# S5 stage: input and scan-operator loads set ahead of output operators, both swaps of a pair ahead of its scans, loads lent the idle weight buffers

## The chip, the cores and the metric

One Trainium2 core runs the whole program. The metric is the device time of one launch in microseconds (us), as the median of repeated runs. TensorE multiplies matrices (PE; its weight loads are PEld), VectorE (DVE) and ScalarE (ACT) do elementwise work, GpSimd (POOL) does small fills and issues some DMAs, SyncE (SP) issues most DMAs. Each engine takes its own instructions in order.

## What is computed

A two-layer decoder trunk on x of 512 tokens by 1024 features, all in fp32. Layer 0 is FFN, Mamba-2 mixer, FFN; layer 1 is FFN, S5 mixer, FFN. The change is in the S5 mixer alone:

```
lam_bar = exp(lam * step);  b_bar = ((lam_bar - 1) / lam) * b
u = rmsnorm(x).reshape(L, 64 groups, 16)
h[t] = lam_bar * h[t-1] + b_bar @ u[t]          (64 complex states a group)
y[t] = real(c @ h[t]) + d * u[t];  g = gelu(y)
val, gate = split(g @ glu_w + glu_b);  x = x + val * sigmoid(gate)
```

## The kernel before

**Stages.** `f1_0, ssd, f2_0, f1_1, s5, f2_1` run one after the other. An fp32 product is taken as three matmuls of rounded halves (hi*hi, hi*lo, lo*hi; lines 235 to 237). In the FFNs the weight halves lie in the pools `whi` and `wlo`, three buffers each of 128 x 8 x 128 fp32; inside the S5 stage nothing needs them until the GLU weights 4 and up are split.

**S5 in tiles.** The 64 groups are cut into eight blocks i of eight groups, worked in pairs (0,1), (2,3), (4,5), (6,7). Time is cut into 64 steps of 8 tokens. For a block:

- `u_load(i)` fetches the block's input U (128 x 8 x 64) from a DRAM scratch `d_u`, in runs of 64 fp32; `scan_ops(i, n)` fetches the operator `opH` and, for n = 2, the table `tb`, into a ring of five buffers; `out_ops(i, h)` fetches the output operators `opP`, half h, into five buffers. All go through SP's queue.
- `states(i)`: DVE multiplies U by the norm's factor (line 1401), then 16 pairs of matmuls on PE give the step inputs in PSUM (line 1407).
- `scan(i)`: ACT copies the two halves of that PSUM tile crosswise into z2 (the *swap*, lines 1417 and 1418); DVE forms z1 and z2 with the table (1419, 1420), adds them (1421), runs the recurrence (1423), and after two more crosswise copies on ACT (1427, 1428) rotates the states back: v1 = z*tb, z2*tb, v1 - z2 (1429 to 1431). POOL fills rh and the first column of v1.
- `mix(i, h, w)` for a pair (i, i+1), half h: PE adds the direct part from U (w = 128) and the part from v1 (w = 0) (line 1440); ACT takes the gelu (1448).
- `channels(i)`: PE transposes the pair's gelu output (1460), ACT and DVE cut it into halves gh and gl (1464, 1465).
- `glu_k(i)`: twelve matmuls that add block i into four GLU outputs, whose weights are resident. GLU weights 4 and up (`glu_load`, POOL's queue) are split on ACT (226) and DVE (228).

**Order.** In this stage the order on PE, SP and POOL is the order of the code; on ACT and DVE a scheduler chooses it when the program is built. PE's order is states 0, 1; mix 0 (U); states 2; mix 0 (v); states 3; channels 0; then for the pairs from (4,5): states of the pair, mix of the pair before, two glu_k, channels. `ahead(i)` issues the loads: the four opP of pair (i, i+1), and behind them U, opH and tb of the next pair. An opP buffer comes free when the mix that read it is done. PSUM lends this stage four `aux` tiles.

Of the kernel before, what the change touches and what calls it, by code (L numbers as in the profile page):

```python
# [9 lines left out]
F32 = mybir.dt.float32  # L10
# [6 lines left out]
T = 512  # L17
D = 1024
KD = 8
# [11 lines left out]
def trunk_kernel(ctx, tc, x, ffn1_norm, ffn1_w_in, ffn1_w_out, mix_norm, ffn2_norm, ffn2_w_in, ffn2_w_out,  # L31
# [3 lines left out]
    nc = tc.nc  # L35
    V, S, G, PE = nc.vector, nc.scalar, nc.gpsimd, nc.tensor

    const = ctx.enter_context(tc.tile_pool(name="const", bufs=1))
    wpool = ctx.enter_context(tc.tile_pool(name="wpool", bufs=3))
# [8 lines left out]
    def aux_ps():  # L48
        return psum.tile([128, 512], F32, tag="aux", name="aux", bufs=4)
# [59 lines left out]
    def col(nm, j=0, n=1):  # L109
        i, r0 = C[nm]  # L110
        return cols[i][:, r0 + j:r0 + j + n]
# [864 lines left out]
    s5 = {}  # L976
# [347 lines left out]
    fl = lambda a: a.rearrange("p g k -> p (g k)")  # L1324
    gs8 = lambda i: slice(i * 8, i * 8 + 8)
    s5_in, s5_out = {}, {}
# [3 lines left out]
    def scan_ops(i, n):  # L1330

        w = s5_w.setdefault(i, [])
        while len(w) < n:
            if w:
                t_ = s5["ring"].tile([128, 2, 8, 64], F32, tag="ut", name="tb", bufs=5)
                nc.sync.dma_start(t_, s5["t"][i])
            else:
                t_ = s5["ring"].tile([128, 8, 128], F32, tag="ut", name="opH", bufs=5)
                nc.sync.dma_start(t_, s5["H"][:, gs8(i)])
            w.append(t_)  # L1340
        return w

    def u_load(i):

        if i not in s5_in:
            U = s5["op"].tile([128, 8, 64], F32, name="U", bufs=4)
            nc.sync.dma_start(U, s5["u"][i].rearrange("(g c) q k -> (c q) g k", c=16))
            s5_in[i] = U
        return s5_in[i]

    def out_ops(i, h):

        if (i, h) not in s5_out:
            P_ = s5["op"].tile([128, 4, 256], F32, name="opP", bufs=5)
            nc.sync.dma_start(P_, s5["P"][:, i * 8 + h * 4:i * 8 + h * 4 + 4])
            s5_out[i, h] = P_
        return s5_out[i, h]
# [32 lines left out]
    def s5_stage(pr, nxt):  # L1390
        with ExitStack() as es:
            sp = es.enter_context(tc.tile_pool(name="s5", bufs=2))
# [3 lines left out]
            pbs, ins, pys = {}, {}, {}  # L1396

            def states(i):

                U, W = u_load(i), scan_ops(i, 1)[0]  # L1400
                V.tensor_tensor(U, U, rL[:, None, :].to_broadcast([128, 8, 64]), op=OP.mult)
                pb = pbs[i] = aux_ps()
                for g in range(8):
                    s = slice(g * 64, g * 64 + 64)
                    for hf in range(2):
                        m = slice(hf * 64, hf * 64 + 64)
                        PE.matmul(pb[m, s], W[:, g, m], U[:, g], start=True, stop=True)

            def scan(i):

                pb, tb = pbs[i], scan_ops(i, 2)[1]
                rh = sp.tile([128, 8, 64], F32, name="rh", bufs=2)
                G.memset(rh[:, :, 0:1], 0.0)
                G.tensor_copy(rh[:, :, 1:], s5["rho"][:, gs8(i)][:, :, None].to_broadcast([128, 8, 63]))
                z1 = sp.tile([128, T], F32, name="z1", bufs=1)
                z2 = sp.tile([128, 8, 64], F32, name="z2")
                S.copy(fl(z2)[0:64], pb[64:128])
                S.copy(fl(z2)[64:128], pb[0:64])
                V.tensor_tensor(z1, pb, fl(tb[:, 0]), op=OP.mult)
                V.tensor_tensor(fl(z2), fl(z2), fl(tb[:, 1]), op=OP.mult)  # L1420
                V.tensor_tensor(z1, z1, fl(z2), op=OP.add)
                z = sp.tile([128, 8, 64], F32, name="z", bufs=1)
                V.tensor_tensor_scan(fl(z), fl(rh), z1, 0.0, op0=OP.mult, op1=OP.add)
                v1 = ins[i] = sp.tile([128, 8, 64], F32, name="v1", bufs=3)
                v2 = sp.tile([128, 8, 64], F32, name="z2")
                G.memset(v1[:, :, 0:1], 0.0)
                S.copy(v2[0:64, :, 1:64], z[64:128, :, 0:63])
                S.copy(v2[64:128, :, 1:64], z[0:64, :, 0:63])
                V.tensor_tensor(v1[:, :, 1:64], z[:, :, 0:63], tb[:, 0, :, 0:63], op=OP.mult)
                V.tensor_tensor(v2[:, :, 1:64], v2[:, :, 1:64], tb[:, 1, :, 0:63], op=OP.mult)  # L1430
                V.tensor_tensor(v1[:, :, 1:64], v1[:, :, 1:64], v2[:, :, 1:64], op=OP.subtract)

            def mix(i, h, w):

                if w:
                    pys[i, h] = aux_ps()
                py = pys[i, h]
                for g in range(4):
                    for e in range(2):
                        PE.matmul(py[e * 64:e * 64 + 64, g * 128:g * 128 + 128],  # L1440
                                  (u_load(i + e) if w else ins[i + e])[:, h * 4 + g],
                                  out_ops(i + e, h)[:, g, w:w + 128], start=bool(w) and g == 0,
                                  stop=not w and g == 3, skip_group_check=True)
                if w:
                    return
                if h == 0:
                    pys["gy"] = sp.tile([128, 8, 8, 16], F32, name="gy", bufs=1)
                S.activation(pys["gy"][:, :, h * 4:h * 4 + 4].rearrange("p q g c -> p g q c"),
                             py.rearrange("p (g q c) -> p g q c", g=4, q=8), AF.Gelu_apprx_tanh)
# [19 lines left out]
            def glu_k(i):  # L1469
                for j in range(2 * NR):  # L1470
                    hi, lo = res[j]
                    proj(rps[j], (hi[i // 4][:, i % 4:i % 4 + 1], lo[i // 4][:, i % 4:i % 4 + 1]), GH[i:i + 1],
                         GL[i:i + 1], first=i == 0, last=i == KD - 1)

            def glu_out(d, pv, pg):
                sg = sp.tile([128, T], F32, tag="z2", name="sg")
                S.activation(sg, pg, AF.Sigmoid, bias=col("gb", 8 + d))
                V.scalar_tensor_tensor(sg, pv, col("gb", d), sg, op0=OP.add, op1=OP.mult)
                new = s5.pop("spare")
                xv, sv = [a_.rearrange("p (q k) -> p k q", q=8) for a_ in (xT[d], sg)]  # L1480
                V.tensor_tensor(new.rearrange("p (k q) -> p k q", q=8), xv, sv, op=OP.add)
                s5["spare"], xT[d] = xT[d], new
                nxt.take(d)
                if d == KD - 1:
                    S.copy(s5["spare"], xT[1])
                    xT[1] = s5["spare"]

            def ahead(i):

                if i < KD:  # L1490
                    for h in range(2):
                        out_ops(i, h)
                        out_ops(i + 1, h)
                if i + 2 < KD:
                    for j in (i + 2, i + 3):
                        u_load(j)
                        scan_ops(j, 2)

            raw = {}

            def glu_load(*js):
                for j in js:
                    raw[j] = fetch_w(glu_cols(j), KD, eng=G)[0]
# [2 lines left out]
                states(i)  # L1506
            for h in range(2):
                mix(0, h, 128)
            scan_ops(2, 2)
            scan_ops(3, 1)  # L1510
            scan(0)
            scan(1)
            scan_ops(3, 2)
            states(2)
            for h in range(2):
                mix(0, h, 0)
            states(3)
            ahead(2)
            scan(2)
            channels(0)  # L1520
            scan(3)
            for i in range(4, KD + 2, 2):
                if i < KD:
                    states(i)
                    states(i + 1)
                for h in range(2):
                    mix(i - 2, h, 128)
                    mix(i - 2, h, 0)
                ahead(i)
                if i < KD:  # L1530
                    scan(i)
                    scan(i + 1)
                if i == KD - 2:
                    glu_load(4, 5)
                glu_k(i - 4)
                glu_k(i - 3)
                channels(i - 2)
# [7 lines left out]
            for d in range(NR):  # L1545
                glu_out(d, rps[2 * d], rps[2 * d + 1])
# [64 lines left out]
    with tc.manual_schedule(engines={mybir.EngineType.Activation, mybir.EngineType.DVE, mybir.EngineType.PE}):  # L1611
        xps, w = {}, {}
# [75 lines left out]
    for i, s in enumerate(stages[:-1]):  # L1688
# [5 lines left out]
        elif s == "s5":  # L1694
            with tc.manual_schedule(engines={mybir.EngineType.PE, mybir.EngineType.SP, mybir.EngineType.Pool}):
                s5_stage(pr, nxt)
# [75 lines left out]
```

## Time and profile before

| | |
|---|---|
| timed runs | 2053.25 us median of 3 (2051.19 to 2054.72) |
| the profiled execution | 2049.33 us, its span 2047.6 us, mean granted clock 0.989 |
| busy over the span | PE 1990.9 us, DVE 1494.4, ACT 943.5, POOL 223.3 |
| S5 stage | PE's first state matmul at 1537.09 us, its transposes of the last pair at 1611.45 us |

Times in the text are us from the start of the span. A row of the timeline reads: start, length, engine, line, operation, output <- input, shape, count, and in brackets the idle time before it with what ended it. A row of the chain of waits reads: start, length, what ran or what was waited for. A row of a table by windows gives busy time and count by engine (PE, PEld, DVE, ACT, POOL), the granted TensorE clock, the DMA share and the GB/s.

### The profile page before, as it was taken

How to read it: one execution, taken by the hardware profiler on the slowest of the kernel's cores; microseconds unless marked ns; L12 is line 12 of the kernel's file. 1: busy time of each engine (PE TensorE's matmuls, PEld its weight loads, DVE VectorE, ACT ScalarE, POOL GpSimd, SP SyncE). 2: the span in 40 equal slices, each digit the busy share in tenths (PEclk: the TensorE clock that was granted, in tenths of full speed). 3: DMA queues.
4: the chain of work that ended last, by engine and by line, in shares of the span. 5: the costliest groups of instructions: out<-in, count | busy, mean ns of one | idle time of the engine just before them, and what ended most of it. 6: DMA issues, size and time to landing. Idle time of an engine off the chain costs nothing. (4 is left out here: it accounts for less than half of the span.)

```text
span 2047.6 us, 32113 instructions
## 1 busy us (share of the span) xinstructions
PE 1990.9 (97%) x12477; PEld 1730.1 (84%) x12477; DVE 1494.4 (73%) x2677; ACT 943.5 (46%) x1613; POOL 223.3 (11%) x338
## 2 busy tenths in 40 slices
PE   8999999999999999999999999999985999999997
PEld 7887778888888887889999978999975888999996
DVE  6899986687875787776676667666767556866675
ACT  5324334465663565444444534444444433444453
POOL 1002322012111010000011000000101100100010
PEclk9999999999999999999999999999997999999999
DMA  7446675343334322355566327455766432654561
GB/s 188 121 122 166 166 192 129 96 118 121 111 101 121 103 84 68 106 148 122 120 149 153 93 85 171 118 120 128 189 197 218 132 103 72 166 138 112 131 141 67
DMA packets 410057, 265.47 MB, mean 130 GB/s; under 512 B 40008, under 2 KB 383088, under 8 KB 409904
## 3 DMA queue, kind: packets, MB, share of 16 engines
q1 hardware_dynamic: 383024, 202.60, 35.4%
q0 software_dynamic: 26560, 59.75, 14.0%
q8 instruction: 98, 1.61, 0.3%
q10 hardware_dynamic: 320, 1.06, 0.1%
q14 instruction: 55, 0.45, 0.1%
HBM read 215.06 MB, written 21.04 MB: 115 GB/s over the span
## 5 line engine op out<-in xcount | busy, mean ns | idle before, releaser
L226 ACT CAST whi<-wst 128x1024 fp32r<-128x1024 f32 (+3 forms) x354 | 315.5, 893 | 380.0 <-PE mm L236 291.2
L228 DVE TENSOR_TENSOR wlo<-wst,whi 128x1024 fp32r<-128x1024 f32 (+3 forms) x354 | 363.8, 1028 | 125.1 <-ACT whi L226 123.4
L235 PE MATMUL mm<-hH,whi 128*128 128x512 f32 x984 | 389.8, 396 | 0.0
L236 PE MATMUL mm<-hL,whi 128*128 128x512 f32 x984 | 384.6, 391 | 1.8 <-DVE hL L182 1.7
L237 PE MATMUL mm<-hH,wlo 128*128 128x512 f32 x984 | 383.9, 390 | 0.0
L237 PE MATMUL mm<-ah,wlo 128*128 128x512 f32 x704 | 274.8, 390 | 0.0
L235 PE MATMUL mm<-ah,whi 128*128 128x512 f32 x704 | 274.5, 391 | 0.0
L236 PE MATMUL mm<-al,whi 128*128 128x512 f32 x704 | 274.4, 390 | 0.0
L236 PEld LDWEIGHTS mm<-hL,whi 128*128 128x128 f32 x984 | 185.2, 188 | 41.1 <-DVE hL L182 3.0
L237 PEld LDWEIGHTS mm<-hH,wlo 128*128 128x128 f32 x984 | 184.9, 188 | 39.7 <-DVE wlo L228 0.4
L235 PEld LDWEIGHTS mm<-hH,whi 128*128 128x128 f32 x984 | 185.0, 188 | 39.4 <-issue 1.6
L384 PE MATMUL mm<-th,hH 128*128 128x256 f32 x612 | 173.5, 284 | 0.0
L386 PE MATMUL mm<-th,hL 128*128 128x256 f32 x612 | 173.2, 283 | 0.0
L385 PE MATMUL mm<-tl,hH 128*128 128x256 f32 x612 | 173.1, 283 | 0.0
L237 PEld LDWEIGHTS mm<-ah,wlo 128*128 128x128 f32 x704 | 132.2, 188 | 27.9 <-issue 0.6
L236 PEld LDWEIGHTS mm<-al,whi 128*128 128x128 f32 x704 | 132.3, 188 | 26.6 <-issue 0.2
L235 PEld LDWEIGHTS mm<-ah,whi 128*128 128x128 f32 x704 | 132.3, 188 | 26.0
L299 POOL DMA_DIRECT2D wu<-wst x51 | 43.2, 847 | 829.5 <-DMA wst<-in_ffn_w_in_dram 266.6
L384 PEld LDWEIGHTS mm<-th,hH 128*128 128x128 f32 x612 | 117.4, 192 | 2.4 <-ACT up L458 2.4
L385 PEld LDWEIGHTS mm<-tl,hH 128*128 128x128 f32 x612 | 117.4, 192 | 0.0
L386 PEld LDWEIGHTS mm<-th,hL 128*128 128x128 f32 x612 | 117.4, 192 | 0.0
L386 PE MATMUL mm<-th,wlo 128*128 128x256 f32 x408 | 115.5, 283 | 0.0
(393 smaller groups left out, 3918.9 us busy)
## 6 DMA issues: line engine op xcount, KB each, us to landing
wst<-in_ffn_w_in_dram SPq DMA_DIRECT2D x125, 512.0 KB, 4.5
wu<-in_ffn_w_in_dram SPq DMA_DIRECT2D x51, 512.0 KB, 5.9
wst<-in_ssd_in_proj_dram SPq DMA_DIRECT2D x48, 512.0 KB, 3.9
wst<-in_ffn_w_out_dram SPq DMA_DIRECT2D x72, 256.0 KB, 2.9
wst<-in_ffn_w_out_dram SPq DMA_DIRECT2D x48, 320.0 KB, 3.2
wu<-wst POOLq DMA_DIRECT2D x51, 256.0 KB, 4.5
ws<-wst POOLq DMA_DIRECT2D x51, 256.0 KB, 4.7
dec<-d_cs POOLq DMA_DIRECT2D x16, 512.0 KB, 4.5
```

The source lines that it names most:

```text
L226: S.copy(hi, st)
L228: V.tensor_tensor(lo, st, hi.bitcast(F32), op=OP.subtract)
L235: PE.matmul(ps, hi[:, k], H[k], start=first and k == 0, stop=False)
L236: PE.matmul(ps, hi[:, k], L[k], start=False, stop=False)
L237: PE.matmul(ps, lo[:, k], H[k], start=False, stop=last and k == n - 1)
L299: G.dma_start(dst, src, accum_op=OP.add)
L384: PE.matmul(ps[:, c0], hi[:, k], mh, start=first and k == 0, stop=False, skip_group_check=True)
L385: PE.matmul(ps[:, c0], hi[:, k], ml, start=False, stop=False, skip_group_check=True)
L386: PE.matmul(ps[:, c0], lo[:, k], mh, start=False, stop=k == 3, skip_group_check=True)
```

## The change

In SP's queue U and opH of blocks 4 and 5 are issued right behind the loads of blocks 2 and 3, ahead of opP for pair (2,3); the loads of 6 and 7 follow that opP, and `ahead` is left as `next_out`, which loads opP alone. opH of 4 and 5 and both U of 6 and 7 go into the three `whi` buffers, opH of 6 and both tables of 6 and 7 into the three `wlo` buffers. `swap(i)` is cut out of `scan(i)`, and both swaps of a pair are called ahead of its two scans; z2 gets three buffers instead of two. PE's order stays. Line numbers move: 1401 is 1407, 1407 is 1413, 1417 to 1431 are 1424 to 1445, 1440 is 1454, 1465 is 1479.

```diff
@@ -1331,19 +1331,25 @@
 
         w = s5_w.setdefault(i, [])
         while len(w) < n:
-            if w:
-                t_ = s5["ring"].tile([128, 2, 8, 64], F32, tag="ut", name="tb", bufs=5)
-                nc.sync.dma_start(t_, s5["t"][i])
+            nm, shape = ("tb", [128, 2, 8, 64]) if w else ("opH", [128, 8, 128])
+            tag = {(4, 0): "whi", (5, 0): "whi", (6, 0): "wlo", (6, 1): "wlo", (7, 1): "wlo"}.get((i, len(w)))
+            if tag:
+                t_ = wpool.tile(shape, F32, tag=tag, name=nm, bufs=3)
             else:
-                t_ = s5["ring"].tile([128, 8, 128], F32, tag="ut", name="opH", bufs=5)
-                nc.sync.dma_start(t_, s5["H"][:, gs8(i)])
+                t_ = s5["ring"].tile(shape, F32, tag="ut", name=nm, bufs=5)
+            nc.sync.dma_start(t_, s5["t"][i] if w else s5["H"][:, gs8(i)])
             w.append(t_)
         return w
 
     def u_load(i):
 
         if i not in s5_in:
-            U = s5["op"].tile([128, 8, 64], F32, name="U", bufs=4)
+            if i < 6:
+                U = s5["op"].tile([128, 8, 64], F32, name="U", bufs=4)
+            elif i == 6:
+                s5_in["last"] = wpool.tile([128, 2, 8, 64], F32, tag="whi", name="U", bufs=3)
+            if i >= 6:
+                U = s5_in["last"][:, i - 6]
             nc.sync.dma_start(U, s5["u"][i].rearrange("(g c) q k -> (c q) g k", c=16))
             s5_in[i] = U
         return s5_in[i]
@@ -1406,23 +1412,31 @@
                         m = slice(hf * 64, hf * 64 + 64)
                         PE.matmul(pb[m, s], W[:, g, m], U[:, g], start=True, stop=True)
 
-            def scan(i):
-
-                pb, tb = pbs[i], scan_ops(i, 2)[1]
+            swapped = {}
+
+            def swap(i):
+
+                pb = pbs[i]
                 rh = sp.tile([128, 8, 64], F32, name="rh", bufs=2)
                 G.memset(rh[:, :, 0:1], 0.0)
                 G.tensor_copy(rh[:, :, 1:], s5["rho"][:, gs8(i)][:, :, None].to_broadcast([128, 8, 63]))
-                z1 = sp.tile([128, T], F32, name="z1", bufs=1)
-                z2 = sp.tile([128, 8, 64], F32, name="z2")
+                z2 = sp.tile([128, 8, 64], F32, name="z2", bufs=3)
                 S.copy(fl(z2)[0:64], pb[64:128])
                 S.copy(fl(z2)[64:128], pb[0:64])
+                swapped[i] = rh, z2
+
+            def scan(i):
+
+                pb, tb = pbs[i], scan_ops(i, 2)[1]
+                rh, z2 = swapped[i]
+                z1 = sp.tile([128, T], F32, name="z1", bufs=1)
                 V.tensor_tensor(z1, pb, fl(tb[:, 0]), op=OP.mult)
                 V.tensor_tensor(fl(z2), fl(z2), fl(tb[:, 1]), op=OP.mult)
                 V.tensor_tensor(z1, z1, fl(z2), op=OP.add)
                 z = sp.tile([128, 8, 64], F32, name="z", bufs=1)
                 V.tensor_tensor_scan(fl(z), fl(rh), z1, 0.0, op0=OP.mult, op1=OP.add)
                 v1 = ins[i] = sp.tile([128, 8, 64], F32, name="v1", bufs=3)
-                v2 = sp.tile([128, 8, 64], F32, name="z2")
+                v2 = sp.tile([128, 8, 64], F32, name="z2", bufs=3)
                 G.memset(v1[:, :, 0:1], 0.0)
                 S.copy(v2[0:64, :, 1:64], z[64:128, :, 0:63])
                 S.copy(v2[64:128, :, 1:64], z[0:64, :, 0:63])
@@ -1473,7 +1487,7 @@
                          GL[i:i + 1], first=i == 0, last=i == KD - 1)
 
             def glu_out(d, pv, pg):
-                sg = sp.tile([128, T], F32, tag="z2", name="sg")
+                sg = sp.tile([128, T], F32, tag="z2", name="sg", bufs=3)
                 S.activation(sg, pg, AF.Sigmoid, bias=col("gb", 8 + d))
                 V.scalar_tensor_tensor(sg, pv, col("gb", d), sg, op0=OP.add, op1=OP.mult)
                 new = s5.pop("spare")
@@ -1485,16 +1499,12 @@
                     S.copy(s5["spare"], xT[1])
                     xT[1] = s5["spare"]
 
-            def ahead(i):
+            def next_out(i):
 
                 if i < KD:
                     for h in range(2):
                         out_ops(i, h)
                         out_ops(i + 1, h)
-                if i + 2 < KD:
-                    for j in (i + 2, i + 3):
-                        u_load(j)
-                        scan_ops(j, 2)
 
             raw = {}
 
@@ -1506,16 +1516,30 @@
                 states(i)
             for h in range(2):
                 mix(0, h, 128)
+            swap(0)
+            swap(1)
+            scan(0)
+            scan_ops(3, 1)
             scan_ops(2, 2)
-            scan_ops(3, 1)
-            scan(0)
             scan(1)
+            for i in (4, 5):
+                u_load(i)
+                scan_ops(i, 1)
             scan_ops(3, 2)
+            out_ops(2, 0)
+            scan_ops(4, 2)
             states(2)
             for h in range(2):
                 mix(0, h, 0)
             states(3)
-            ahead(2)
+            swap(2)
+            swap(3)
+            next_out(2)
+            scan_ops(5, 2)
+            for i in (6, 7):
+                u_load(i)
+            for i in (6, 7):
+                scan_ops(i, 2)
             scan(2)
             channels(0)
             scan(3)
@@ -1526,8 +1550,10 @@
                 for h in range(2):
                     mix(i - 2, h, 128)
                     mix(i - 2, h, 0)
-                ahead(i)
+                next_out(i)
                 if i < KD:
+                    swap(i)
+                    swap(i + 1)
                     scan(i)
                     scan(i + 1)
                 if i == KD - 2:
```

SP's queue behind the load of U for block 3, up to U of block 5, before (d_u4 and d_u5 are the inputs of blocks 4 and 5; the number behind tb's source is that block's table):

```order
L1336 DMA tb_15394<-d_t2_121 128x1024
L1339 DMA opH_15396<-d_H_117 128x1024
L1336 DMA tb_15438<-d_t3_122 128x1024
L1355 DMA opP_15495<-d_P_118 128x1024
L1355 DMA opP_15497<-d_P_118 128x1024
L1355 DMA opP_15499<-d_P_118 128x1024
L1355 DMA opP_15501<-d_P_118 128x1024
L1347 DMA U_15503<-d_u4_15083 128x8x64
L1339 DMA opH_15505<-d_H_117 128x1024
L1336 DMA tb_15507<-d_t4_123 128x1024
L1347 DMA U_15509<-d_u5_15084 128x8x64
```

The same queue from the same place, now:

```order
L1340 DMA opH_15420<-d_H_117 128x1024
L1340 DMA tb_15422<-d_t2_121 128x1024
L1353 DMA U_15438<-d_u4_15083 128x8x64
L1340 DMA opH_15440<-d_H_117 128x1024
L1353 DMA U_15442<-d_u5_15084 128x8x64
L1340 DMA opH_15444<-d_H_117 128x1024
L1340 DMA tb_15446<-d_t3_122 128x1024
L1361 DMA opP_15448<-d_P_118 128x1024
L1340 DMA tb_15450<-d_t4_123 128x1024
L1361 DMA opP_15519<-d_P_118 128x1024
L1361 DMA opP_15521<-d_P_118 128x1024
L1361 DMA opP_15523<-d_P_118 128x1024
```

U of 4 and 5 have moved from behind the four opP to the third and fifth place; behind the last opP now stand tb of 5, U of 6 and 7 and their operators.

DVE's queue from the scan of block 1 on, before (15430 is v1 of block 1, 15527 v1 of block 2, tb_14982 the table of block 1 and tb_15394 that of block 2):

```order
L1423 SCALAR_TENSOR_TENSOR z_15428<-rh_15418,z1_15421 128x512
L1429 TENSOR_TENSOR v1_15430<-z_15428,tb_14982 128x8x63
L1430 TENSOR_TENSOR z2_15431<-z2_15431,tb_14982 128x8x63
L1431 TENSOR_TENSOR v1_15430<-v1_15430,z2_15431 128x8x63
L1419 TENSOR_TENSOR z1_15518<-aux_15441,tb_15394 128x512
L1420 TENSOR_TENSOR z2_15519<-z2_15519,tb_15394 128x512
L1421 TENSOR_TENSOR z1_15518<-z1_15518,z2_15519 128x512
L1423 SCALAR_TENSOR_TENSOR z_15525<-rh_15515,z1_15518 128x512
L1429 TENSOR_TENSOR v1_15527<-z_15525,tb_15394 128x8x63
```

From the same operation, now (15430 is again v1 of block 1, U_15438 and U_15442 are the inputs of blocks 4 and 5):

```order
L1437 SCALAR_TENSOR_TENSOR z_15428<-rh_15400,z1_15424 128x512
L1443 TENSOR_TENSOR v1_15430<-z_15428,tb_14982 128x8x63
L1407 TENSOR_TENSOR U_15438<-U_15438,nw5_y_15313 128x512
L1444 TENSOR_TENSOR z2_15431<-z2_15431,tb_14982 128x8x63
L1433 TENSOR_TENSOR z1_15538<-aux_15453,tb_15422 128x512
L1434 TENSOR_TENSOR z2_15510<-z2_15510,tb_15422 128x512
L1445 TENSOR_TENSOR v1_15430<-v1_15430,z2_15431 128x8x63
L1435 TENSOR_TENSOR z1_15538<-z1_15538,z2_15510 128x512
L1407 TENSOR_TENSOR U_15442<-U_15442,nw5_y_15313 128x512
L1437 SCALAR_TENSOR_TENSOR z_15542<-rh_15507,z1_15538 128x512
```

The multiplication of U for block 4 now stands inside the scan of block 1, that of block 5 ahead of the recurrence of block 2, and the end of block 1's scan is mixed with the start of block 2's.

ACT's queue around the swap of block 3, before (15528 takes the crosswise copies of block 2's states, 15561 is the swap of block 3):

```order
L1448 ACTIVATE gy_15466<-aux_15376 128x4x8x16
L1427 COPY z2_15528<-z_15525 64x8x63
L1428 COPY z2_15528<-z_15525 64x8x63
L1448 ACTIVATE gy_15466<-aux_15385 128x4x8x16
L1417 COPY z2_15561<-aux_15478 64x512
L1418 COPY z2_15561<-aux_15478 64x512
```

And now (15545 takes the copies of block 2's states, 15516 is the swap of block 3):

```order
L1462 ACTIVATE gy_15478<-aux_15376 128x4x8x16
L1462 ACTIVATE gy_15478<-aux_15385 128x4x8x16
L1424 COPY z2_15516<-aux_15490 64x512
L1425 COPY z2_15516<-aux_15490 64x512
L1441 COPY z2_15545<-z_15542 64x8x63
L1442 COPY z2_15545<-z_15542 64x8x63
```

The swap of block 3 has gone ahead of the copies that finish block 2.

## The prediction

> **What bounds the kernel now.** A gain is to be had where PE, the engine that carries most of the work, waits. I read PE's waits first, in the stretch that the change touches, 1536 to 1612 us (columns: total us, times, longest).
>
> ```profile
> PE aux L1407 <- DVE U L1401: 11.0, 3, 5.7
> PE aux L1440 <- DVE v L1431: 8.5, 2, 5.6
> PE aux L1407 <- DVE gl L1465: 7.9, 2, 5.3
> ```
>
> In all 27.4 us of PE waiting. From 1612 to 1760, the rest of the stage and on into the last FFN, the same view has one row:
>
> ```profile
> PE mm L236 <- DVE hL L182: 0.3, 1, 0.3
> ```
>
> So what is won before 1612 is not given back to a wait there. The timeline of PE says which of the 27.4 us the change can reach (states are L1407, mix is L1440, glu_k is L235 to L237, transposes L1460):
>
> ```profile
> 1537.09 3.68 PE L1407 MATMUL aux<-U,opH 128*64 128x64 f32 x64 [5.70 <-DVE U L1401]
> ...
> 1540.56 2.16 PE L1440 MATMUL aux<-opP,U 128*64 128x128 f32 x32
> ...
> 1552.51 3.43 PE L1440 MATMUL aux<-opP,v 128*64 128x128 f32 x29 [5.60 <-DVE v L1431]
> ...
> 1564.27 1.98 PE L1407 MATMUL aux<-U,opH 128*64 128x64 f32 x32 [5.25 <-DVE gl L1465]
> 1568.26 1.97 PE L1407 MATMUL aux<-U,opH 128*64 128x64 f32 x32 [2.01 <-DVE U L1401]
> 1569.99 1.93 PE L1440 MATMUL aux<-opP,U 128*64 128x128 f32 x16
> 1571.70 1.09 PE L1440 MATMUL aux<-opP,v 128*64 128x128 f32 x16
> ...
> 1574.47 0.50 PE L235 MATMUL mm<-gh,hH 128*128 128x512 f32 x1
> ...
> 1580.05 1.03 PE L1460 MATMUL aux<-ident,gy 128*128 128x128 f32 x8
> 1583.76 1.15 PE L1407 MATMUL aux<-U,opH 128*64 128x64 f32 x32 [2.68 <-DVE gl L1465]
> 1588.20 1.97 PE L1407 MATMUL aux<-U,opH 128*64 128x64 f32 x32 [3.29 <-DVE U L1401]
> 1589.93 1.95 PE L1440 MATMUL aux<-opP,U 128*64 128x128 f32 x16
> ...
> 1594.67 0.50 PE L235 MATMUL mm<-gh,hH 128*128 128x512 f32 x1
> ...
> 1601.21 1.09 PE L1440 MATMUL aux<-opP,U 128*64 128x128 f32 x16
> ...
> 1604.86 0.49 PE L235 MATMUL mm<-gh,hH 128*128 128x512 f32 x1
> 1605.52 0.50 PE L236 MATMUL mm<-gl,hH 128*128 128x512 f32 x1 [0.17 <-DVE gl L1465]
> ...
> 1608.81 0.50 PE L236 MATMUL mm<-gl,hH 128*128 128x512 f32 x1 [0.25 <-DVE gl L1465]
> ...
> 1611.45 1.03 PE L1460 MATMUL aux<-ident,gy 128*128 128x128 f32 x8
> ```
>
> The wait before 1537.09 is the norm's and stays. Those of 5.25, 2.01, 2.68 and 3.29 us, 13.2 together, stand before the states of blocks 4 to 7. The chain of waits names what ended last there, the input U:
>
> ```profile
> 1556.17 6.69 DMA U<-d_u
> ...
> 1574.93 7.38 DMA U<-d_u
> ```
>
> U of block 4 was issued at 1556.17 and U of block 6 at 1574.93 because SP's queue held four opP loads ahead of them, which wait for the mix before:
>
> ```profile
> 1546.04 10.08 SPq L1355 DMA_DIRECT2D opP<-d_P  x4
> ```
>
> **The change part by part.** All times below stand against this one execution, 2049.33 us; the median of the timed runs, 2053.25, lies 3.92 above, and I carry the difference over. Rows of DVE give the prices:
>
> ```profile
> 1543.69 0.68 DVE L1429 TENSOR_TENSOR v<-z,tb 128x504 f32<-128x504 f32 x1
> ...
> 1548.38 1.23 DVE L1423 TENSOR_TENSOR_SCAN z<-rh,z 128x512 f32<-128x512 f32 x1
> 1549.64 0.68 DVE L1429 TENSOR_TENSOR v<-z,tb 128x504 f32<-128x504 f32 x1
> 1550.96 0.68 DVE L1430 TENSOR_TENSOR z<-z,tb 128x504 f32<-128x504 f32 x1 [0.64 <-ACT z L1428]
> 1551.68 0.68 DVE L1431 TENSOR_TENSOR v<-v,z 128x504 f32<-128x504 f32 x1
> ...
> 1559.16 0.69 DVE L1419 TENSOR_TENSOR z<-aux,tb 128x512 f32<-128x512 f32 x1 [0.79 <-ACT z L1418]
> 1559.77 0.68 DVE L1420 TENSOR_TENSOR z<-z,tb 128x512 f32<-128x512 f32 x1
> ...
> 1564.15 1.21 DVE L1423 TENSOR_TENSOR_SCAN z<-rh,z 128x512 f32<-128x512 f32 x1
> ...
> 1567.92 0.68 DVE L1431 TENSOR_TENSOR v<-v,z 128x504 f32<-128x504 f32 x1
> ...
> 1580.55 0.68 DVE L1431 TENSOR_TENSOR v<-v,z 128x504 f32<-128x504 f32 x1
> ```
>
> From start to start an operation costs 0.6 us, 0.7 when it takes the result just before, the recurrence 1.26; a pair of crosswise copies keeps the last product until 1.3 after the recurrence ended.
>
> *Blocks 0 to 3: nothing gained.* From 1543.69 six operations now stand ahead of the recurrence of block 1 (6 x 0.6), which starts at 1547.3 instead of 1548.38, because the swap of block 1 is done and fills the wait for ACT. But behind it come the multiplication of U for block 4 (0.6) and two operations of block 2, the first of which waits for its swap on ACT, so the last subtraction of block 1 starts at 1552.3 instead of 1551.68: 0.6 late. PE's mix of pair (0,1), the states of block 3 and its swap follow 0.6 late, and z1 of block 3 starts at 1559.75 instead of 1559.16. Since that swap stands ahead of block 2's copies, the rest of block 2 and four half-width gl come after it; the recurrence of block 3 starts at 1564.0 and its last subtraction, with the multiplication of U for block 6 ahead of it, at 1567.75: 0.2 early.
>
> *U of 4 and 5.* Their issue now waits only for the mix of pair (0,1) with U, done by 1542.7 (1540.56 + 2.16). U's loads took this long to land (us, least, median, most):
>
> ```profile
> DMA to landing us min/median/max: 4.8/7.2/8.9
> ```
>
> Here opH of 3 and tb of 2 stand ahead in the queue, and opP stood ahead of the load of 6.69, so I take 6.5 and a landing at 1549.2, just when DVE asks for U at 1549.15. For U of 5, 8 us behind 1543.7, that is 1551.7 against 1553.4. Both ends stay for the range: at 4.8 nothing changes, at 8.9 DVE stands still for 2.5 us. Two rows of the table by windows, the first without a U under way, the second with one:
>
> ```profile
> 1548.00:1550.00 2.00, 0.00 (x0) 0.00 (x0) 1.86 (x3) 0.30 (x1) 0.33 (x2) 0.50 0.92 344
> 1562.00:1564.00 2.00, 0.00 (x0) 0.00 (x0) 1.12 (x3) 0.00 (x0) 0.00 (x0) 0.50 1.03 399
> ```
>
> The rate does not fall with U's short runs, 344 against 399 GB/s. The Trainium skill, DMA: Bandwidth & Descriptors, Specifications, speaks against the change here: a transfer needs runs of at least 512 B for the full rate, and U's runs are 256 B. By that rule U would land at the long end, 8.9, and the gain below would be 7.4 us; by the rows it is 9.4, and I keep the rows.
>
> *Pair (2,3) on PE.* The states of 4 and 5 and the first part of the mix (two L1407 of 1.98, then 1.93) now run behind the eight transposes of pair (0,1), from 1559.7 on, while DVE works on block 3, and are done when its v1 is ready at 1568.5. That part of the mix then starts at 1568.5 instead of 1571.70, 3.2 early. PE paused about 3 us before it; the window from 1562 shows the clock at 0.50 after such a pause, so the remaining three parts may cost up to 4.4 us instead of 2.8 (1571.70 to 1574.47). They end between 1571.3 and 1572.9.
>
> *Pair (4,5).* Two glu_k 5.6 (1574.47 to 1580.05), transposes 0.9, two warm states 1.15 each without the waits of 2.68 and 3.29: PE reaches its mix between 1580.1 and 1581.7. DVE: from 1568.35, where that subtraction of block 3 makes room, fourteen operations, two of them recurrences (12 x 0.6 and 2 x 1.26), and 1.1 of waits for copies and for the result just before, lead to block 5's last subtraction at 1579.15 instead of 1580.55; then gl of pair (2,3) frees a PSUM tile at 1581. So the mix starts at about 1581.4 instead of 1589.93. At 3.9 us (the warm mix from 1601.21 to 1604.86 took 3.65) it ends at 1585.3 instead of 1594.67: 9.3 early.
>
> *Pair (6,7).* Two glu_k, transposes and the U part bring PE to 1592.7. DVE, free of gl at 1581.4, waits for the swap of block 6 and starts z1 at 1582.65; two interleaved scans take 10.1, so v1 of block 7 is ready at 1593.5. PE waits 0.8, a new wait, and the mix ends at 1596.3 instead of 1604.86. The split of GLU weight 4 follows the mix of (4,5), since POOL issues its load behind a fill that waits for that mix:
>
> ```profile
> 1595.43 3.61 POOL L217 DMA_DIRECT2D wst<-in_s_glu_w_dram  x4 [0.53 <-issue]
> ```
>
> ```profile
> 1602.50 1.04 ACT L226 CAST whi<-wst 128x1024 fp32r<-128x1024 f32 x1 [4.51 <-DMA wst<-in_s_glu_w_dram]
> ```
>
> It came 7.8 us after 1594.67; now at 1593.1, and the two rounded halves and gl of block 4 by 1596.0, in time. With the two stalls at 1605.52 and 1608.81 gone (6.6 us become 5.75), the transposes of the last pair start at 1602.0 instead of 1611.45. **Gain 9.4 us**; none of it is lost behind 1612: 2049.33 - 9.4 = 2039.9, and 2053.25 - 9.4 = 2043.8 on the median.
>
> *Lent buffers, a third z2, POOL's fills:* nothing. The last FFN matmul read the halves long before 1542, and the first GLU halves are wanted by PE at 1603, 8 us after they are made. Cover gone, their cost would be that of a late split, us for us.
>
> **The rivals.** *A late U in DVE's queue.* U of 4, 5 and 6 stand inside scans, where a late load holds everything behind it, which was no danger when U stood behind the scan. At 8.9 us U of 4 costs 2.5 at 1549.2, some of it covered by the wait for the swap: gain 7.4, time 2045.9. For: opH and tb of three blocks now share the queue. Against: the DMA share of 0.92 at 1548 was followed by an idle queue. Chance 0.13.
>
> *Hidden anyway.* PE's waits named gl, not only U, so PSUM tiles could bind the states of 4 and 5, and the scans go no faster. Then only block 6's late U is won, the 2.68 and 3.29: gain 6.0, time 2047.3. For: v1 of blocks 3 and 5 come only 0.2 and 1.4 earlier. Against: v1 of 3 was ready 3 us before PE used it. Chance 0.13.
>
> *Slower: the loads run one after the other.* If U of 4 waits for opH and tb ahead of it and U of 5 for U and opH of 4, each at 8.9 to land in turn, U of 5 holds the recurrence of block 2 until about 1561 and costs about 3. It decides against the change when the hold passes 9.4 us, so when U of 5, asked for at 1553.4, lands later than 1562.8, 19 us after its issue; at a landing of 1566.9 the hold is 13.5 and the kernel takes 2057.3. Against: the longest landing is 8.9. Chance 0.04.
>
> **How the numbers follow.** The forecast has 0.70: 2043.8, by itself 2041.0 to 2046.0, since the prices of some forty operations of DVE in a row may each be off by 0.05 us, 2 in all, and a slow clock takes back part of 1.6. With the first two rivals the range that holds 8 in 10 is 2040.5 to 2048.8. About 0.2% (4.1 us) is what a measurement of this kernel can tell from no change. Faster by more is the forecast, the late U and most of the hidden case: 0.70 + 0.12 + 0.08 = 0.90. Within 0.2% are their tails: 0.07. Slower: 0.03 of the last rival.
>
> **What would show it.** Right: no wait for U before the states of 4 to 7; v1 of block 3 ready near 1568.5 and PE's mix of (2,3) directly behind it; the mix of (4,5) ending 9 us early; a short new wait for v1 of block 7. Wrong: an idle DVE in front of a multiplication of U, waits of PE for gl before the states of 5, or the transposes of the last pair later than 1606.

## The result and the profile after

| | before | after |
|---|---|---|
| timed runs, us | 2052.22 median of 4 (2050.81 to 2054.72) | 2041.18 median of 4 (2039.9 to 2043.6) |
| the profiled execution, us | 2049.33, span 2047.6 | 2039.9, span 2038.0 |
| first state matmul to the transposes of the last pair, us | 1537.09 to 1611.45: 74.36 | 1537.62 to 1601.92: 64.30 |

The ratio of the timed runs is 0.9948, with a 95% interval from 0.9935 to 0.9961: 8.0 to 13.3 us faster than before, 11.0 by the medians. The spans differ by 9.6.

Between executions the first state matmul starts anywhere from 1536.3 to 1541.6 us, for reasons that lie ahead of this stage (last section). A span therefore carries up to 5 us that the change did not make. So the traces are compared by the third row, the *stage length*: 10.06 us shorter. From those transposes to the end of the span it is 436.15 us before (2047.6 - 1611.45) and 436.08 after: all of the gain reaches the end.

PE's waits in the stage, after (total us, times, longest):

```profile
PE aux L1454 <- DVE v L1445: 12.4, 4, 4.9
PE aux L1413 <- DVE U L1407: 5.8, 1, 5.8
PE aux L1454 <- issue: 2.3, 1, 2.3
```

20.5 us instead of 27.4. (Before, the view has a fourth row, 0.4 us for the two stalls in the last glu_k.) The 5.8 is the wait ahead of the stage, which was 5.70. The four waits for U and gl before the states of blocks 4 to 7 (13.2 us) are gone; the wait for v1 grew from 8.5 to 12.4, and 2.3 are new. The timeline of PE, after, shows where:

```profile
1537.62 3.68 PE L1413 MATMUL aux<-U,opH 128*64 128x64 f32 x64 [5.81 <-DVE U L1407]
...
1548.30 0.66 PE L1454 MATMUL aux<-opP,v 128*64 128x128 f32 x2 [4.23 <-DVE v L1445]
1553.87 3.43 PE L1454 MATMUL aux<-opP,v 128*64 128x128 f32 x29 [4.91 <-DVE v L1445]
...
1559.88 2.24 PE L1413 MATMUL aux<-U,opH 128*64 128x64 f32 x64
1564.45 1.25 PE L1454 MATMUL aux<-opP,U 128*64 128x128 f32 x16 [2.34 <-issue]
1565.42 0.63 PE L1454 MATMUL aux<-opP,v 128*64 128x128 f32 x2
1568.86 1.73 PE L1454 MATMUL aux<-opP,v 128*64 128x128 f32 x13 [2.81 <-DVE v L1445]
...
1573.17 0.50 PE L235 MATMUL mm<-gh,hH 128*128 128x512 f32 x1
...
1579.72 2.08 PE L1413 MATMUL aux<-U,opH 128*64 128x64 f32 x64
1581.63 1.05 PE L1454 MATMUL aux<-opP,U 128*64 128x128 f32 x16
...
1585.23 0.50 PE L235 MATMUL mm<-gh,hH 128*128 128x512 f32 x1
...
1593.59 0.95 PE L1454 MATMUL aux<-opP,v 128*64 128x128 f32 x13 [0.51 <-DVE v L1445]
...
1596.32 0.50 PE L235 MATMUL mm<-gh,hH 128*128 128x512 f32 x1
...
1601.92 1.03 PE L1474 MATMUL aux<-ident,gy 128*128 128x128 f32 x8
```

The states of 4 and 5, and of 6 and 7, are now one row of 64 matmuls each without a bracket. Apart from the 2.34 us that the profile calls "issue", PE now waits for v1 alone, that of blocks 0, 1, 3 and 7.

Waiting explains only 7.0 us of the 10.06 (21.7 us beside the first wait, now 14.7). Most of the other 3 us is work that no longer stands behind a wait and so runs at a higher clock. States of 4 and 5: 3.95 us before, 2.24 now. States of 6 and 7: 3.12, now 2.08. The mix of (4,5): 4.74 (1589.93 to 1594.67), now 3.60 (1581.63 to 1585.23). These three gain 3.9. The last two glu_k take 5.60 instead of 6.59; that is not the clock, which was 1.00 both times, but the end of their stalls, in which matmuls and weight loads waited for gl. Against these 4.9, the mix of (2,3) is 1.4 dearer, 5.91 us in two pieces (1564.45 to 1566.05 and 1568.86 to 1573.17) instead of 4.48 (1569.99 to 1574.47), because waits are there now; 0.4 are lost in smaller pieces. So the clock's share, 3.9 less 1.4, is about 2.5 us net. In a table by windows the granted clock is the third number from the end. Before, with the states of block 4 in it:

```profile
1564.00:1566.00 2.00, 1.73 (x32) 1.76 (x32) 1.97 (x3) 0.55 (x1) 0.58 (x2) 0.50 1.18 312
```

And after, the first row with the states of blocks 4 and 5 in it:

```profile
1560.00:1562.00 2.00, 2.00 (x64) 1.90 (x64) 1.78 (x3) 1.94 (x5) 0.00 (x0) 1.00 0.84 295
1562.00:1564.00 2.00, 0.12 (x4) 0.00 (x0) 2.00 (x6) 0.86 (x3) 0.00 (x0) 1.00 1.05 334
1564.00:1566.00 2.00, 1.55 (x18) 1.23 (x18) 2.00 (x5) 0.43 (x1) 0.46 (x2) 0.82 0.82 170
1566.00:1568.00 2.00, 0.06 (x1) 0.00 (x0) 1.89 (x3) 1.95 (x4) 0.25 (x2) 0.50 0.72 162
...
1570.00:1572.00 2.00, 2.00 (x22) 2.00 (x21) 1.90 (x4) 0.60 (x1) 0.00 (x0) 0.50 1.02 416
```

Behind PE's pauses of 2.34 and 2.81 us the clock falls to 0.50, and most of the mix of (2,3) runs at it.

DVE's timeline, after:

```profile
1549.92 1.09 DVE L1407 TENSOR_TENSOR U<-U,nw_y 128x512 f32<-128x512 f32 x1
...
1553.05 0.68 DVE L1445 TENSOR_TENSOR v<-v,z 128x504 f32<-128x504 f32 x1
...
1560.22 0.69 DVE L1433 TENSOR_TENSOR z<-aux,tb 128x512 f32<-128x512 f32 x1 [3.44 <-ACT z L1425]
...
1563.93 0.42 DVE L1479 TENSOR_TENSOR gl<-aux,gh 128x256 fp32r<-128x256 f32 x1
...
1567.44 0.69 DVE L1407 TENSOR_TENSOR U<-U,nw_y 128x512 f32<-128x512 f32 x1
1568.04 0.68 DVE L1445 TENSOR_TENSOR v<-v,z 128x504 f32<-128x504 f32 x1
```

U of block 4 is there when DVE asks for it (no bracket at 1549.92). The largest hole is the 3.44 us before z1 of block 3, which waits for its swap: the states of block 3 stand on PE behind the v part of mix (0,1), and that waits for v1 of block 1.

The issue of loads on SP, after:

```profile
1543.17 0.37 SPq L1353 DMA_DIRECT2D U<-d_u  x1
...
1558.07 0.99 SPq L1353 DMA_DIRECT2D U<-d_u  x2
1559.11 6.89 SPq L1340 DMA_DIRECT2D opH<-d_H  x1
```

and how long U of 4 and 5, and behind them U of 6 and 7, took to land, after (us from the issue):

```profile
DMA to landing us min/median/max: 4.0/5.0/6.1
```

```profile
DMA to landing us min/median/max: 9.0/9.2/9.4
```

U of block 4 is issued at 1543.17 instead of 1556.17 and lands in 4.0 us, at 1547.2, while DVE asks for it at 1549.92. U of block 6 is issued at 1558.07 instead of 1574.93, takes 9.0, and is there at 1567.1. DVE multiplies it at 1567.44. That is 0.3 to 0.4 us in hand, with the last subtraction of block 3 right behind it in DVE's queue.

### The profile page after: what moved, and what is told of

Same layout as the page of the kernel before. It is cut to its first block, busy times and chain, and to the rows that moved or that the text cites. A ratio compares the mean times of both kernels' runs of the same rounds, so it can differ in the third digit from the quotient of the medians.

```text
span 2038.0 us, 32117 instructions
## 1 busy us (share of the span) xinstructions
PE 1988.1 (98%) x12477; PEld 1727.5 (85%) x12477; DVE 1493.7 (73%) x2677; ACT 943.4 (46%) x1613; POOL 223.9 (11%) x338
## 3 DMA queue, kind: packets, MB, share of 16 engines
q1 hardware_dynamic: 383024, 202.60, 35.5%
## 5 line engine op out<-in xcount | busy, mean ns | idle before, releaser
L385 PE MATMUL mm<-tl,whi 128*128 128x256 f32 x408 | 115.5, 283 | 0.0
```

What stands on the lines that cost most here:

```text
L385: PE.matmul(ps[:, c0], hi[:, k], ml, start=False, stop=False, skip_group_check=True)
```

## The experiments

All are edits of the kernel after. The kernel before was timed beside them: 2053.28 us in the first four (e1, e2, e3, e5), 2053.7 in the last four.

| kernel | median, us | ratio to before, 95% interval | stage, us | length |
|---|---|---|---|---|
| e1, loads alone | 2044.02 | 0.996 (0.9947 to 0.9972) | 1536.33 to 1601.57 | 65.24 |
| e2, swaps alone | 2052.33 | 1.0002 (0.9993 to 1.0011) | 1540.70 to 1615.83 | 75.13 |
| e3, loads of 4, 5 and swaps | 2047.08 | 0.9977 (0.9968 to 0.9986) | 1540.72 to 1608.98 | 68.26 |
| e4, loads of 6, 7 and swaps | 2044.52 | 0.9958 (0.9945 to 0.997) | 1541.60 to 1610.00 | 68.40 |
| e5, states of 3 ahead of mix (0,1) | 2036.84 | 0.9929 (0.9915 to 0.9943) | 1541.19 to 1601.86 | 60.67 |
| e6, U of 4 and 5 later | 2041.39 | 0.9942 (0.9929 to 0.9954) | 1541.27 to 1605.82 | 64.55 |
| e7, e5 and e6 together | 2038.17 | 0.9929 (0.9916 to 0.9943) | 1536.83 to 1598.46 | 61.63 |
| the change again | 2044.13 | 0.9948 (0.9935 to 0.996) | 1537.03 to 1601.23 | 64.20 |

The last row says how far a stage length can be trusted: two executions of the same kernel give 64.30 and 64.20. Its expectation was:

> The change itself once more, to have it beside the others: stage length 64 to 65 us, 8 to 12 us faster than before.

**The loads without the swaps.** Each swap is put back right ahead of its own scan.

```diff
             swap(0)
-            swap(1)
             scan(0)
...
+            swap(1)
             scan(1)
...
+            swap(2)
             scan(2)
             channels(0)
+            swap(3)
             scan(3)
...
                     swap(i)
+                    scan(i)
                     swap(i + 1)
-                    scan(i)
                     scan(i + 1)
```

> The loads are moved as in the change, each swap stays right ahead of its own scan. Theory (the early U carries the gain): no wait for U before the states of blocks 4 to 7, and 7 to 10 us faster than before, at most 2 us slower than the change, since two scans of 6 us in a row replace two interleaved ones of 5.4. Rival (the swaps carry it, the scans on VectorE being the bound): at most 4 us faster than before.

The stage is 65.24 us, 9.12 shorter than before: the loads alone carry nine tenths of the change. PE's timeline:

```profile
1565.90 1.73 PE L1454 MATMUL aux<-opP,v 128*64 128x128 f32 x13 [2.98 <-DVE v L1445]
...
1593.25 0.95 PE L1454 MATMUL aux<-opP,v 128*64 128x128 f32 x13 [1.58 <-DVE v L1445]
```

Counted from the stage's start, v1 of block 3 is taken at 29.6 us, earlier than the change's 31.2 (1568.86 - 1537.62): between blocks 0 and 3 the swaps first are a loss. In the last pair they are a gain: the wait for v1 of block 7 is 1.58 us here, 0.51 in the change. The second is what is left at the end, 65.24 against 64.30. These 0.9 us rest on the traces: by the medians e1, at 2044.02, cannot be told from the change, which has 2041.18 and 2044.13.

**The swaps without the loads.** SP's order and the buffers are those of before.

```diff
-            tag = {(4, 0): "whi", (5, 0): "whi", (6, 0): "wlo", (6, 1): "wlo", (7, 1): "wlo"}.get((i, len(w)))
+            tag = None
...
+                if i + 2 < KD:
+                    for j in (i + 2, i + 3):
+                        u_load(j)
+                        scan_ops(j, 2)
...
-            for i in (4, 5):
-                u_load(i)
-                scan_ops(i, 1)
...
-            for i in (6, 7):
-                u_load(i)
-            for i in (6, 7):
-                scan_ops(i, 2)
```

> Both swaps of a pair go ahead of its scans as in the change, the loads stay where they were before. Theory (the early U carries the gain): U of block 4 and of block 6 are again issued behind four opP, TensorE waits for them as before, and the time is within 2 us of before. Rival (the swaps carry it): 5 us or more faster than before.

No change that can be measured: ratio 1.0002, stage 75.13 against 74.36. PE's timeline shows why:

```profile
1566.98 1.98 PE L1408 MATMUL aux<-U,opH 128*64 128x64 f32 x32 [5.69 <-DMA opH<-d_H]
1571.71 1.97 PE L1408 MATMUL aux<-U,opH 128*64 128x64 f32 x32 [2.75 <-DVE U L1402]
...
1587.49 1.15 PE L1408 MATMUL aux<-U,opH 128*64 128x64 f32 x32 [2.15 <-DVE gl L1474]
1591.93 1.98 PE L1408 MATMUL aux<-U,opH 128*64 128x64 f32 x32 [3.29 <-DVE U L1402]
```

All four waits before the states of 4 to 7 are back, 13.9 us in all (13.2 before). The first is now put down to the DMA of opH, not to gl. A load stood behind that wait before, too, and not that of U alone: opH of block 4, issued at 1556.64, took 7.5 us to land, until 1564.1, and gl was done at 1564.23. By that, U of block 4 set early without its opH would have won little; it was not tried.

**One pair's loads at a time.** The loads of 4 and 5 early, those of 6 and 7 behind opP as before (e3); and the reverse (e4). The swaps stay as in the change.

```diff
+                if i == 4:
+                    for j in (i + 2, i + 3):
+                        u_load(j)
+                        scan_ops(j, 2)
...
-            for i in (6, 7):
-                u_load(i)
-            for i in (6, 7):
-                scan_ops(i, 2)
```

> The change, but the loads of blocks 6 and 7 stay behind the opP loads of pair (4,5), in the buffers they had before. Theory: the states of blocks 4 and 5 come without a wait, the mix of (2,3) ends 1.5 to 3 us early, and U of block 6 is issued that much earlier; its landing, 7.4 us behind, still comes 1 to 3 us after TensorE is ready, and of block 7 somewhat later: 3 to 6 us faster than before. Rival (only the late U of block 6 was ever paid): under 2 us faster.

```diff
+                if i == 2:
+                    for j in (i + 2, i + 3):
+                        u_load(j)
+                        scan_ops(j, 2)
...
-            for i in (4, 5):
-                u_load(i)
-                scan_ops(i, 1)
             scan_ops(3, 2)
-            out_ops(2, 0)
-            scan_ops(4, 2)
...
-            scan_ops(5, 2)
```

> The change, but the loads of blocks 4 and 5 stay behind the opP loads of pair (2,3), in the buffers they had before; those of 6 and 7 follow them. By stage length (first state matmul to the transposes of the last pair; before 74.4 us, the change 64.3, only blocks 4 and 5 early 68.3). Theory: the states of 4 and 5 wait as before, those of 6 and 7 come directly behind the transposes, which takes away 2.68 and 3.29 us and leaves a wait of 1 to 2 us for v1 of block 7: 67 to 69 us. As only 4 and 5 early gained 6.1, the two halves then do not add up to 10.1, since TensorE's wait moves from one pair to the next. Rival (only the first late U is paid, the second hides): 72 us or more.

The first is 6.1 us shorter than before, the second 6.0, together more than the change's 10.06. PE's timelines, first with the loads of 4 and 5 alone:

```profile
1583.53 1.15 PE L1408 MATMUL aux<-U,opH 128*64 128x64 f32 x32 [0.34 <-DVE U L1402]
1586.74 1.98 PE L1408 MATMUL aux<-U,opH 128*64 128x64 f32 x32 [2.06 <-DVE z L1428]
```

and with those of 6 and 7 alone:

```profile
1569.43 1.97 PE L1413 MATMUL aux<-U,opH 128*64 128x64 f32 x32 [7.77 <-DMA opH<-d_H]
1574.09 1.97 PE L1413 MATMUL aux<-U,opH 128*64 128x64 f32 x32 [2.69 <-DVE U L1407]
...
1587.99 2.08 PE L1413 MATMUL aux<-U,opH 128*64 128x64 f32 x64
```

Each half takes away the waits before its own pair's states. The halves don't add up because the first shortens the last pair's waits too, from 6.0 us to 2.4, so that less is left for the second to take. The second half alone is, loads for loads, what the prediction's rival "hidden anyway" priced at 6.0.

**Where the next wait comes from.** The states of block 3, and with them its swap, are set ahead of the v part of mix (0,1), so that z1 of block 3 no longer depends on v1 of block 1.

```diff
             states(2)
-            for h in range(2):
-                mix(0, h, 0)
             states(3)
             swap(2)
             swap(3)
+            for h in range(2):
+                mix(0, h, 0)
```

> The change, with the states of block 3 and both swaps of pair (2,3) ahead of the part of the first mix that needs v1 of blocks 0 and 1. In the trace of the change VectorE stood idle for 3.44 us before z1 of block 3, because the swap of block 3 waited for its states, and these for that mix. Theory: this idle time goes, v1 of block 3 is ready about 3 us earlier, and as TensorE waits for it, the kernel is 2 to 3.5 us faster than the change, 12 to 14 us faster than before. Rival (it is TensorE's own work and not the scans that sets the pace from the mix of (2,3) on): within 1 us of the change.

The stage is 60.67 us, 3.6 below the change and just past the expected 2 to 3.5, and the median 2036.84. PE's timeline:

```profile
1550.05 1.15 PE L1413 MATMUL aux<-U,opH 128*64 128x64 f32 x32 [1.85 <-issue]
...
1567.35 1.09 PE L1454 MATMUL aux<-opP,U 128*64 128x128 f32 x16 [0.23 <-PE aux L1413]
1568.25 1.13 PE L1454 MATMUL aux<-opP,v 128*64 128x128 f32 x16
...
1581.35 1.09 PE L1454 MATMUL aux<-opP,U 128*64 128x128 f32 x16 [1.66 <-issue]
```

and DVE's:

```profile
1560.27 0.68 DVE L1433 TENSOR_TENSOR z<-aux,tb 128x512 f32<-128x512 f32 x1
...
1567.50 0.67 DVE L1445 TENSOR_TENSOR v<-v,z 128x504 f32<-128x504 f32 x1
```

DVE's hole of 3.44 us is closed, and block 3's last subtraction starts 26.3 us into the stage instead of 30.4. PE's waits of 2.34 and 2.81 in the mix of (2,3) are gone, so that each of its parts of 16 matmuls takes 1.1 us. A new wait of 1.66 stands before the mix of (4,5). That the profiled span is 2038.0, no shorter than the change's, comes from the stage's start, 3.6 us later here.

**U of 4 and 5 later.** Both are issued behind tb of 3, the first opP of (2,3) and tb of 4.

```diff
-            for i in (4, 5):
-                u_load(i)
-                scan_ops(i, 1)
             scan_ops(3, 2)
             out_ops(2, 0)
             scan_ops(4, 2)
+            for i in (4, 5):
+                u_load(i)
+                scan_ops(i, 1)
             states(2)
```

> The change, but U of blocks 4 and 5 is issued behind the table of block 3, the first opP, opH and the table of block 4, some 5 us later; VectorE then takes their multiplications in its pause before z1 of block 3 and not inside the scans of blocks 1 and 2. Theory (U of 4 and 5 has room to come later, and its multiplication inside the scan of block 1 costs 0.6 us): the last subtraction of block 1 0.6 us earlier, the states of 4 and 5 wait less than 1 us, stage length 63.5 to 64.5 us. Rival (the landing of U of 4 has no room, every microsecond of its issue is paid): 67 us or more.

The stage is 64.55, 0.25 and 0.35 above the change's two and just past the expected 64.5. DVE's timeline:

```profile
1560.40 0.69 DVE L1407 TENSOR_TENSOR U<-U,nw_y 128x512 f32<-128x512 f32 x1 [0.74 <-DMA U<-d_u]
1561.41 0.69 DVE L1407 TENSOR_TENSOR U<-U,nw_y 128x512 f32<-128x512 f32 x1 [0.32 <-DMA U<-d_u]
...
1570.67 0.69 DVE L1407 TENSOR_TENSOR U<-U,nw_y 128x512 f32<-128x512 f32 x1 [1.35 <-DMA U<-d_u]
1571.28 0.68 DVE L1445 TENSOR_TENSOR v<-v,z 128x504 f32<-128x504 f32 x1
```

The program's order on DVE came out anew: the multiplications of U for 4 and 5 moved out of the scans into DVE's pause before z1 of block 3, and the last subtraction of block 1 starts 13.7 us into the stage (1555.01) instead of 15.4. What that wins is lost again. DVE stands still for 0.74 and 0.32 us for U of 4 and 5, whose landing took 8.0 and 8.5 us here, and for 1.35 for U of block 6 in the middle of block 3's scan. That load took this long (U of 6, U of 7):

```profile
DMA to landing us min/median/max: 9.4/9.6/9.8
```

Little longer than in the change, but DVE asks for it 8.0 us after its issue (1561.28 to 1569.32), not 9.4 (1558.07 to 1567.44). Behind it stands the last subtraction of block 3, for which PE waits:

```profile
1572.10 1.73 PE L1454 MATMUL aux<-opP,v 128*64 128x128 f32 x13 [4.05 <-DVE v L1445]
```

This is the late U of the prediction's first rival, seen in a run: of the 1.7 us that the last subtraction of block 1 is ahead, 0.4 are left at that of block 3, 30.0 us into the stage instead of 30.4, and the hold was 1.35. The clock takes the rest: behind a wait of 4.05 instead of 2.81 the last part of the mix takes 1.99 us for 15 matmuls, 1.13 in the change.

**Both together.** e5's order with e6's loads:

> States of block 3 and both swaps of pair (2,3) ahead of the first mix with v1, and U of blocks 4 and 5 issued behind the table of block 3, the first opP, opH and the table of block 4. By stage length the former alone took 60.7 us. Theory (the multiplication of U of 4 inside the scan of block 1 is on the path until the mix of (0,1)): 59.5 to 60.3 us. Rival (with VectorE's pause gone, U of 4 and 5 now lands after VectorE or TensorE wants it): 61 us or more.

61.63 us: better than the change by 2.6, but worse than e5 alone by 1.0, and outside the 59.5 to 60.3 of the theory. The time is the rival's, its reason is not. The multiplications of U stand inside the scans again, and DVE waits for none of them. PE's timeline has two waits that e5 did not have, or not as long:

```profile
1559.42 1.15 PE L1413 MATMUL aux<-U,opH 128*64 128x64 f32 x32 [1.26 <-DVE U L1407]
...
1577.35 1.36 PE L1454 MATMUL aux<-opP,U 128*64 128x128 f32 x16 [1.97 <-issue]
```

The first of them costs nothing: the last subtraction of block 3 starts 26.3 us into the stage in both kernels, and the transposes of pair (2,3) 35.5. The loss lies behind the second. The mix of (4,5) starts 0.4 later than in e5, and the granted clock falls to 0.50 in it, so that its four parts take 1.36, 1.99, 1.72 and 1.07 us. In e5, behind a wait of 1.66, the clock stayed at 1.00 and they take 1.09, 1.07, 1.07 and 1.07. At the transposes of pair (4,5) e7 is 2.0 us behind; in the last pair it does not wait for v1, and 1.0 is left. Why that wait is longer in e7 was not settled. By the timed runs e7 and e5 cannot be told apart (the same ratio and interval), so the 1.0 rests on one stage length each. Against the change, timed beside it on the same chip, e7 is 6.0 us faster by the medians (2038.17 and 2044.13; 2036.45 to 2040.76 against 2039.1 to 2044.25).

A U of block 4 or 5 that lands after DVE wants it, with its multiplication inside a scan of blocks 1 or 2, the prediction's slower rival, was not made: moving the load made DVE's order move with it. So the 19 us after its issue from which that rival decides has not been tried.

## Why the prediction was right

The change was to win 9.4 us and bring the median to 2043.8, with 2041.0 to 2046.0 as the forecast's own range. The median is 2041.18, near the lower end, and the stage gained 10.06. Of the 2.6 us between 2043.8 and 2041.18, 0.7 are the stage's, 1.0 is from the kernel before, whose median is now 2052.22 in place of the 2053.25 that the sum started from, and the rest lies within the spread of the runs.

The predicted times below are given plus 0.53, since the stage started at 1537.62 and not at 1537.09.

*Blocks 0 to 3, nothing gained: held.* The last subtraction of block 1 was put at 1552.8 and came at 1553.05; z1 of block 3 at 1560.3, came at 1560.22; the last subtraction of block 3 at 1568.3, came at 1568.04. Adding up DVE's queue operation by operation, at 0.6 us each, was good to 0.3 us over 25 us.

*U of 4 and 5: held, and the landing was over-sized.* Issue at 1543.2, was 1543.17. The landing was put at 6.5 us, just in time; it took 4.0, with 2.7 us to spare, and 6.1 instead of 8 for U of 5. *U of 6 was not sized at all*, and that was the gap: it took 9.0 and came with 0.3 to 0.4 us to spare (8.4, with 0.9 to spare, in the second execution of the change). The prediction had no figure for it, so that it came in time was luck. The bound of 8.9 that I had for U of 4 was about the right size for U of 6, and e6 shows the price of its coming 1.35 too late.

The rows on the rate, 344 against 399 GB/s, do not stand up. Of the three windows before with a U under way from 1560 to 1566, the prediction took the fastest: they moved 333, 399 and 312 GB/s, at DMA shares of 1.15, 1.03 and 1.18. After, with U of 6 and 7 under way, the window from 1562 moved 334 at a share of 1.05 and the two behind it 170 and 162 at 0.82 and 0.72; the one from 1570, with only other loads under way, moved 416 at 1.02. The Trainium skill, DMA: Bandwidth & Descriptors, Specifications, gives 512 B as the least transfer for the full rate, taken here as the length of a run; the trace leans that way, with a rate a fifth lower and the two U at 9.0 and 9.4 us. What went wrong is what I made of it: U of 4 at 8.9 us and a gain of 7.4, where U of 4 took 4.0 and the stage gained 10.06. No run here varied the length of the runs, so the rule itself is not tested.

*Pair (2,3): held, at its dear end.* The last three parts of the mix were to cost 2.8 to 4.4 us and end by 1573.4. They took 4.31 (1568.86 to 1573.17), for the reason given, the clock at 0.50. Not foreseen were the 2.34 us before the mix's first part. The profile calls them "issue"; the part starts at 1564.45, when a half-width gl of DVE that started at 1563.93 has just ended, so PE was most likely held by a PSUM tile: it starts 0.10 behind the end of that gl, and also 0.10 behind it in the second execution and in e6. It cost nothing, as v1 of block 3 came later still. That is the rival "hidden anyway" in small: its mechanism is there, but it doesn't decide.

*Pair (4,5): held, 0.6 under-sized.* The mix was put at 1581.9 to 1585.8, and ran from 1581.63 to 1585.23. I had taken 3.9 us for it; with no wait ahead of it, it took 3.60, and it began 0.3 sooner. These 0.6 us are the whole difference between the 9.4 forecast and the 10.06 of the stage.

*Pair (6,7): held.* The new wait for v1 of block 7 was to be 0.8, and is 0.51. The mix ends at 1596.32 (1596.8 forecast). The GLU weights came in time: the two stalls in the last glu_k are gone (5.60 us from 1596.32 to 1601.92), and the transposes stand at 1601.92, 0.6 ahead of the forecast. Nothing is lost behind them, nor to the lent buffers: 436.15 us to the end before, 436.08 after.

*Rivals.* The late U did not happen in the change, by 0.3 to 0.4 us; e6 shows it, at 1.35 us for U of block 6. "Hidden anyway" would have needed the states of 4 and 5 to gain nothing; e3 shows that their loads, with the swaps, are worth 6.1. The slower rival did not happen; its own sum does not hold together, as it gives a hold of DVE until 1561, 7.6 us, a cost of about 3, and then lets a hold of 9.4 eat up a gain of 9.4. The timed medians say 11.0 where the stage says 10.06; the interval of 8.0 to 13.3 holds both, and the second comparison, 2044.13 against 2053.7, says 9.6.

*What the prediction left unsaid* is how the gain splits. The loads carry 9.1 of it, the swaps 0.9 and only in the last pair; alone they are worth nothing.

## What to carry to other kernels

When an engine waits for a computed operand, follow it back to the load, and the load back to the queue it was issued in: here the cure was an order of issue, and idle buffers of another stage paid for it. Price the work that follows a wait as well as the wait: about 2.5 of these 10 us were matmuls that no longer ran at half clock, and e7 fell behind e5 in the same way. When the wait is gone, look for the next one on the same path (here a swap that stood behind another pair's mix): closing it was worth another 3.6 us for moving a few lines.

## What the runs showed of the hardware

- The issue of a load can itself hold SP. That of opH for block 6 took 6.89 us, right behind the two U (5.46 to 7.12 in the same place of the second execution, e5, e6 and e7; 3.50 at most for opH of blocks 4 to 7 before, with one U right ahead). Two U, in runs of 256 B (128 x 8 runs each), are a tenth of the bytes that moved from 1556 to 1574 and most of the packets:

```profile
DMA packets 3391, 5.35 MB, mean 297 GB/s; under 512 B 2220, under 2 KB 2220, under 8 KB 3388
```

  Two U right ahead are not the whole of it: opH of block 5, behind those of 4 and 5, took 3.77 us in e6 and 2.94 in e7. What holds SP was not tried apart. It cost nothing here: PE took that opH at 1579.72.
- A pause of PE of 2.34 us, from 1562.1, was enough to bring the granted clock down in the window from 1564 (0.82), and it was at 0.50 from 1566, through a second pause of 2.81 and until 1572. The length of a pause alone does not decide: behind 1.97 us in e7 the clock fell, behind 1.66 in e5 it did not, and before, behind 2.68, the states of block 6 still took the 1.15 us of the full clock. A wait of 2 us can have a price behind it, and need not.
- The stage's start varies by 5 us from execution to execution, ahead of all that the change touches. Early or late start goes with the wait before the first state matmul, 5.7 to 5.9 us when it is early (before, both executions of the change, e1, e7) and 3.9 when it is late (e2 to e6). Its cause was not settled; a comparison of two single spans can be off by as much.
